# Output projections whose second accumulator runs a channel step behind the first, with no turn of the recurrence streams in the last steps of the column ahead

## The chip, the cores and the metric

The kernel runs on one core of one Trainium2 chip. A core has TensorE (PE, matrix products into the PSUM banks), VectorE (DVE), ScalarE (ACT), GpSimd (POOL, here only a queue that issues DMAs and a few memsets) and SyncE (SP, which issues the other DMAs). The engines work side by side, each through its own queue of instructions in order, and wait for one another through semaphores. The metric is the device time of one execution in microseconds (us); of several runs the median is given.

## What is computed

A decoder layer on an input of 2048 tokens by 1024 channels, in float32. What matters here is the mixer and its output projection:

```python
h = _rmsnorm(x, norm1_w[l])
proj = h @ w_in[l]                                   # 1024 -> 3840 columns
...
o_hg = _hgrn2_mixer(q_raw, f_raw, i_raw, g_raw, ...) # 4 heads of 128: gated linear recurrence
o_rw = _rwkv7_mixer(r, k, v, wd, ad, gd, ...)        # 8 heads of 64: RWKV-7 time mixing
x = x + jnp.concatenate([o_hg, o_rw], axis=-1) @ w_out[l]   # the output projection
x = x + _conv_ffn(_rmsnorm(x, norm2_w[l]), ...)
...
return _rmsnorm(x, final_norm_w)
```

## The kernel before

The tokens are cut into four blocks of 512. The first phase (`phase1`, L274) makes the input projection, both recurrences and the output projections of blocks 0, 1 and 2; the output projection of block 3 and the feed-forward part follow in the second phase. Every large product is made of three matmuls (`mm3`, L268): both operands are split into a high and a low half of a faster 32-bit format (`wh`, `wl` for weights, `hh`, `hl` for the other operand), and high by high (L270), high by low (L271) and low by high (L272) are added up in one PSUM bank. A split (`split`, L250, `split_to`, L246) is a copy on ScalarE (L254, L247) and a subtraction on VectorE (L255, L248).

Three Python generators write the instructions of phase 1. `rw_stream` (L1143) writes RWKV-7, two supersteps (`rw_super`, L700) for each block, of 42 steps each (41 in the last). `hg_stream` (L1149) writes HGRN2, four units (`hg_unit`, L999) for each block, of 16 steps each. `dense` (L555) writes the dense work: for each block 30 columns of the input projection (eight channel steps of one `mm3` each, into one bank of the tag `pj`, L663 to L679), the transposes for the next block, and the output projections. Projection 0 comes behind the columns of block 1, projection 1 behind those of block 2, and projection 2 at the end of the phase.

The order in which they write is a matter of credit. In each turn of the loop at L1173 both streams write one step. Then `fill` (L1159) gives the dense generator a credit of 2000 ns (`TICK`; times 1.5 or 0.9 in some stretches), and this writes on, paying at each `yield` the number that it yields, until the credit is used up. A column step costs 648 (436 more with a transpose), a step of an output projection 680. The order on each engine's queue is then drawn up when the program is built, from the written order and the dependences; the trace shows that it follows the written order in the main, but not everywhere.

An output projection (`out_block`, L379) has four groups: token half `i2` by column half `dh`. A group has two accumulators, each in a `pj` bank (there are two of that tag in all): `q` = 0 and 1, 128 tokens each, 512 columns. For each of eight channel steps `k` (128 channels) the weights are loaded (by POOL's queue, L393 or L399), split into `wh` and `wl` (four buffers of each, L400), and used by both accumulators, `q` = 0 first (L406 to L415). At the end of a group VectorE adds each bank to the rows of `x` (`xh`, L417), which are stored (L419). In the last group `next_block` (L474) overwrites `hh` and `hl` channel by channel with the next block's input (`split_h`, L463), and at `k` = 3 the weights of the next column are loaded ahead.

The column right ahead of projections 0 and 1 is the gate `g` of the block's last HGRN2 head. Its eviction (`ev_g`, L365) is a sigmoid on ScalarE (`sgm`) and a product on VectorE (`hgg`, L370); these free its `pj` bank. While that column runs, `next_out` (L500) splits the projection's own input, the mixer's output `oT` of two blocks earlier, into `hh` and `hl`, two channels behind the column's matmuls (L677 and L678).

The names of the streams that the text uses: `Af` and `A` are HGRN2's masked score tiles (L1059, L1085 to L1089), made from small matmuls on `hX` (L1045, L1052); `Ti` and `etmp` are RWKV-7's triangular inverse, a long chain of short VectorE operations (L850 to L856).

Of the kernel before, what the change touches and what calls it, by code (L numbers as in the profile page):

```python
# [18 lines left out]
P = 128  # L19
T = 2048  # L20
D = 1024
KD = D // P
# [45 lines left out]
def tile_layer(ctx, tc, consts, x, norm1_w, w_in, hg_lb_logits, hg_norm_w, rw_shift_mu, rw_w0, rw_w2,  # L68
# [177 lines left out]
    def split_to(hi, lo, src):  # L246
        c_ = S.copy(hi, src)  # L247
        return c_, V.tensor_sub(lo, src, hi.bitcast(F32))  # L248

    def split(pool, src, shape, name, bufs):  # L250

        hi = pool.tile(shape, F32R, tag=name + "h", name=name + "h", bufs=bufs)
        lo = pool.tile(shape, F32R, tag=name + "l", name=name + "l", bufs=bufs)
        S.copy(hi, src)  # L254
        V.tensor_sub(lo, src, hi.bitcast(F32))  # L255
        return hi, lo
# [11 lines left out]
    def mm3(acc, lhs, rhs, first, last, skip=False):  # L268
        (lh, ll), (rh, rl) = lhs, rhs
        TE.matmul(acc, lh, rh, start=first, stop=False, skip_group_check=skip)  # L270
        TE.matmul(acc, lh, rl, start=False, stop=False, skip_group_check=skip)  # L271
        TE.matmul(acc, ll, rh, start=False, stop=last, skip_group_check=skip)  # L272

    def phase1(c1):  # L274
        hp = c1.enter_context(tc.tile_pool(name="hp", bufs=1, reuse_waits="tile"))
        wp = c1.enter_context(tc.tile_pool(name="wp", bufs=2, reuse_waits="tile"))
# [17 lines left out]
        hh = hp.tile([P, KD, BLK], F32R, name="hh")  # L294
        hl = hp.tile([P, KD, BLK], F32R, name="hl")

        def bank(kind):
            return ps.tile([P, 512], F32, tag=kind, name=kind, bufs=2)
# [7 lines left out]
        def stg(tag, name, bufs):  # L306
            return sp.tile([P, BLK], F32, tag=tag, name=name, bufs=bufs)
# [71 lines left out]
        def out_block(nb, oh=None, ol=None, then=None, ahead=None):  # L379


            for i2 in range(2):
                for dh in range(2):
                    accs = [bank("pj") for _ in range(2)]
                    for k in range(KD):
                        if i2 == 0 and dh == 1 and oh is not None:
                            split_to(hh[:, k, 256:512], hl[:, k, 256:512], rows["O2"][k // 4][:, k % 4, :])
                        if k % 2 == 0:
                            part_ = 2 * i2 + dh
                            in_s = k < 6 and part_ > (0 if oh is None else 1) or k == 4 and part_ == 0 and oh is None  # L390
                            pair = (sp.tile([P, 2, 512], F32, tag=f"s{k // 2}", name="wpair") if in_s else None)
                            if in_s:
                                wload(pair, w_out[0, k * P:(k + 2) * P, dh * 512:dh * 512 + 512]  # L393
                                      .rearrange("(k p) c -> p k c", p=P))
                        if pair is not None:
                            raw = pair[:, k % 2]
                        else:
                            raw = wp.tile([P, 512], F32, tag="wraw", name="woraw", bufs=4)
                            wload(raw, w_out[0, k * P:(k + 1) * P, dh * 512:dh * 512 + 512])  # L399
                        wh, wl = split(wp, raw, [P, 512], "w", 4)  # L400
                        if k == KD - 2:
                            xh = [stg("sg", "xh", 2) for _ in range(2)]
                            for q in range(2):
                                t0 = nb * BLK + (i2 * 2 + q) * P
                                dma(xh[q], x[0, t0:t0 + P, dh * 512:dh * 512 + 512])
                        for q in range(2):  # L406
                            is_ = slice((i2 * 2 + q) * P, (i2 * 2 + q + 1) * P)
                            lhs = ((hh[:, k, is_], hl[:, k, is_]) if oh is None or i2 == 1 else
                                   (oh[k // 4][:, k % 4, is_], ol[k // 4][:, k % 4, is_]))
                            mm3(accs[q], lhs, (wh, wl), k == 0, k == KD - 1)  # L410
                            if i2 == 1 and dh == 1 and q == 1:
                                next_block(then, k)
                                if k == 3 and ahead is not None:
                                    ahead()
                            yield 680  # L415
                    for q in range(2):
                        V.tensor_add(xh[q], accs[q], xh[q])  # L417
                        r0 = (i2 * 2 + q) * P
                        (nc.gpsimd.dma_start if nb == NBLK - 2 and i2 and dh else dma)(  # L419
                            x1d[nb][r0:r0 + P, dh * 512:dh * 512 + 512], xh[q])  # L420
# [42 lines left out]
        def split_h(nb, k):  # L463

            src, w = rows[nb][:, :, k * P:(k + 1) * P], vec("n1", k)
            h4, l4 = (t_[:, k, :].rearrange("p (i t) -> p i t", i=4) for t_ in (hh, hl))
            act(h4, src, AF.Copy, scale=w)
            V.scalar_tensor_tensor(l4, src, w, h4.bitcast(F32), ALU.mult, ALU.subtract)

        def behind(k):  # L470

            return [k - 2] if 2 <= k < KD - 1 else [k - 2, k - 1, k] if k == KD - 1 else []

        def next_block(nb, k):  # L474

            if nb is not None and nb < NBLK:
                for k_ in behind(k):
                    split_h(nb, k_)
# [76 lines left out]
        def dense():  # L555
# [67 lines left out]
            ahead = iter(())  # L623
            turns = []
            for n, jb in enumerate(jobs):
                if jb[0] == "E":
                    jb[1]()
                    continue
                if jb[0] == "A":
                    if jb[1] == 0:  # L630
                        banks = spread()
                        ahead = transposed(four_tiles(rows[0]), "n1", lambda: next(banks), to_h)
                    continue
                if jb[0] == "T":
                    turns.append(jb[1])
                    continue
                if jb[0] in "OW":
                    while done["rw2"] < 2 * jb[1] + 2 or done["hg"] < 4 * jb[1] + 4:
                        yield None
                    if jb[0] == "W":  # L640
                        jb[2]()
                    else:
                        yield from (out_block(2, *rows["O"]) if jb[1] == 2 else out_block(jb[1], then=jb[1] + 2, ahead=lambda i=i: load(i)))
                    continue
                if jb[0] == "L":
                    while done["rw1"] < 2 * jb[1] + 4 or done["rw2"] < 2 * jb[1] + 2 or done["hg"] < 4 * jb[1] + 4:
                        yield None
                    (o_half if jb[1] == 2 else o_load)(jb[1])
                    continue
                _, col, ev, cond, fin = jb  # L650
                after = jobs[n + 1][1] if jobs[n + 1][0] == "O" and jobs[n + 1][1] < 2 else None
                while not cond():
                    yield None
                load(i)
                ws = loaded.pop(i)
                if i == 0:
                    next(ahead)
                    next(ahead)
                    constants()
                if jobs[n + 1][0] != "O":  # L660
                    load(i + 1)
                i += 1
                acc = bank("pj")  # L663
                then = jobs[n + 1][1] if jobs[n + 1][0] == "A" else None
                for k in range(KD):
                    wh, wl = ws[k // 4]
                    next(ahead, None)
                    mm3(acc, (wh[:, k % 4, :], wl[:, k % 4, :]), (hh[:, k, :], hl[:, k, :]), k == 0, k == KD - 1)
                    aside = k in (1, 5) and len(turns) > 0
                    if aside:  # L670
                        turns.pop(0)()
                    if k == KD - 1:
                        ev(acc)
                        if fin is not None:
                            fin()
                    next_block(then, k)
                    if after is not None:  # L677
                        next_out(after, k)  # L678
                    yield 648 + 436 * aside  # L679

        def last_dma(nb):

# [518 lines left out]
    with ExitStack() as c2:  # L1201
# [36 lines left out]
        with tc.tile_pool(name="op", bufs=1, reuse_waits="tile") as op_:  # L1238
# [61 lines left out]
            for dh in range(2):  # L1300
                accs = [pst("wacc") for _ in range(4)]
                for n, k in enumerate((0, 1, 4, 5, 2, 3, 6, 7)):
                    w = weights(k, dh)
# [15 lines left out]
                    if dh == 1 and 2 <= n:  # L1319
                        for j in range(2):  # L1320
                            q = 2 * (n - 2) + j
# [236 lines left out]
    with tc.tile_pool(name="dn", bufs=1, reuse_waits="tile") as dn:  # L1558
# [53 lines left out]
        accs = {"a": dstate["accs"]}  # L1612
# [7 lines left out]
        for s_ in range(DS, N):  # L1620
# [6 lines left out]
            if s_ < N - 3:  # L1627
                lhs, rhs = ops.pop(s_)
# [53 lines left out]
```

## Time and profile before

| | |
|---|---|
| time, median of 3 runs | 2597.45 us (2592.02, 2597.45, 2602.02) |
| the profiled execution | 2593.87 us, of which 2592.1 us from first to last instruction (the span) |
| mean granted TensorE clock | 0.997 of full speed |
| first matmul of projection 0, 1, 2 | 534.9, 856.7, 1180.0 us after the span's start |
| last matmul of projection 2 | 1258.3 us |
| matmuls of the three projections | 576 (three of 192) |

The profile's page gives busy time by engine, the costliest groups of instructions and the chain of work that ended last. The other views are answers of the trace: the waits of an engine (who waited for whom: sum in us, number, longest), the instructions of an engine in order of time (start, length in us, engine, line, operation, output `<-` inputs, shapes; in brackets the engine's idle time before it and what ended it), and the busy time of every engine in a stretch with the granted clock. A matmul's length in these rows is modelled and overlaps its neighbours'; the distance between starts tells its pace.

### The profile page before, as it was taken

The numbers are of one execution on the slowest core, as the hardware profiler recorded it, in microseconds if no ns is written. First come the engines' busy times: TensorE is split into PE (matmuls) and PEld (weight loads), VectorE is DVE, ScalarE is ACT, GpSimd is POOL, SyncE is SP. The second block draws the span as 40 slices with busy tenths as digits, with TensorE's granted clock in tenths as the row PEclk, the third lists the DMA queues.
The fourth block names the chain that finished last, engine by engine and source line by source line (L and its number), as shares of the span: only waits on it lengthen the run. The fifth ranks groups of instructions, "written<-read, shape, count | busy, mean of one in ns | idle before, by whom it ended". The sixth has DMA issues, their size and how long they took to land.

```text
span 2592.1 us, 50957 instructions
## 1 busy us (share of the span) xinstructions
PE 2526.2 (97%) x19467; PEld 2034.7 (78%) x19467; DVE 1961.6 (76%) x3744; ACT 1381.2 (53%) x2266; POOL 371.4 (14%) x660
## 2 busy tenths in 40 slices
PE   7999999999999999999999999999999999999998
PEld 6777778777777777777788888877888878888887
DVE  4878777685666866788687799988988887666555
ACT  5556554564445644355567644565555454455444
POOL 6433222222222122231000000000000000000000
PEclk9999999999999999999999999999999999999999
DMA  8846455575745657676663477757653564988655
GB/s 310 240 156 192 154 161 146 156 207 176 210 156 159 196 176 196 237 222 171 234 206 126 141 258 252 231 178 232 215 196 101 180 200 134 330 313 289 195 187 191
DMA packets 379722, 518.98 MB, mean 200 GB/s; under 512 B 113887, under 2 KB 210517, under 8 KB 379477
## 3 DMA queue, kind: packets, MB, share of 16 engines
q1 hardware_dynamic: 325361, 337.38, 41.0%
q0 software_dynamic: 54048, 178.32, 21.5%
q8 instruction: 153, 2.51, 0.4%
q14 instruction: 92, 0.75, 0.1%
q10 hardware_dynamic: 68, 0.02, 0.0%
HBM read 372.99 MB, written 134.22 MB: 196 GB/s over the span
## 4 chain that ended last, share of the span: by engine, by line
PE 58%; issue 14%; DVE 12%; DMA 6%; ACT 5%; POOL 4%; SPq 0%; POOLq 0%; DVEq 0%; ACTq 0%
PE pj L270 6%; PE pj L271 5%; PE pj L272 5%; PE ua L270 4%; PE ua L272 4%; PE ua L271 4%; PE da L270 3%; PE da L271 3%; PE da L272 3%; PE db L271 2%; PE db L272 2%; PE db L270 2%; PE ud L272 2%; PE ud L270 2%; PE ud L271 2%
## 5 line engine op out<-in xcount | busy, mean ns | idle before, releaser
L270 PE MATMUL pj<-hh,wh 128*128 128x512 f32 x960 | 394.6, 411 | 1.3 <-ACT xt L122 0.9
L271 PE MATMUL pj<-hl,wh 128*128 128x512 f32 x960 | 378.3, 394 | 0.0
L272 PE MATMUL pj<-hh,wl 128*128 128x512 f32 x960 | 378.0, 394 | 0.0
L270 PE MATMUL ua<-Bh,uwh 128*128 128x512 f32 x704 | 277.0, 393 | 4.0 <-ACT m L122 3.7
L272 PE MATMUL ua<-Bh,uwl 128*128 128x512 f32 x704 | 274.5, 390 | 1.9 <-DVE uwl L255 1.9
L271 PE MATMUL ua<-Bl,uwh 128*128 128x512 f32 x704 | 274.2, 389 | 0.0
L270 PEld LDWEIGHTS pj<-hh,wh 128*128 128x128 f32 x960 | 180.9, 189 | 47.0 <-issue 4.9
L272 PEld LDWEIGHTS pj<-hh,wl 128*128 128x128 f32 x960 | 180.9, 188 | 40.4 <-issue 1.2
L271 PEld LDWEIGHTS pj<-hl,wh 128*128 128x128 f32 x960 | 181.2, 189 | 36.2 <-issue 3.2
L254 ACT CAST uwh<-uraw 128x512 fp32r<-128x512 f32 x220 | 134.5, 617 | 132.6 <-PE ua L271 53.5
L255 DVE TENSOR_TENSOR dal<-draw,dah 128x512 fp32r<-128x512 f32 x138 | 95.2, 690 | 110.9 <-ACT dah L254 110.5
L254 ACT CAST dah<-draw 128x512 fp32r<-128x512 f32 x138 | 85.8, 622 | 164.2 <-PE da L271 77.3
L255 DVE TENSOR_TENSOR uwl<-uraw,uwh 128x512 fp32r<-128x512 f32 x220 | 147.0, 684 | 34.6 <-ACT uwh L254 34.4
L270 PEld LDWEIGHTS ua<-Bh,uwh 128*128 128x128 f32 x704 | 132.1, 188 | 35.9 <-ACT m L122 8.9
L272 PEld LDWEIGHTS ua<-Bh,uwl 128*128 128x128 f32 x704 | 132.2, 188 | 30.5 <-DVE uwl L255 2.8
L271 PEld LDWEIGHTS ua<-Bl,uwh 128*128 128x128 f32 x704 | 132.2, 188 | 26.7
L270 PE MATMUL ud<-Bh,uwh 128*128 128x512 f32 x352 | 138.0, 392 | 0.0
L272 PE MATMUL ud<-Bh,uwl 128*128 128x512 f32 x352 | 137.1, 390 | 0.0
L271 PE MATMUL ud<-Bl,uwh 128*128 128x512 f32 x352 | 137.0, 389 | 0.0
L1552 POOL DMA_DIRECT2D gd<-y x2 | 1.1, 541 | 945.9 <-DVE y L1550 945.9
L271 PE MATMUL da<-dbl,dah 128*128 128x512 f32 x332 | 129.5, 390 | 0.2 <-DVE dbl L255 0.2
L272 PE MATMUL da<-dbh,dal 128*128 128x512 f32 x332 | 129.2, 389 | 0.0
(589 smaller groups left out, 6181.1 us busy)
## 6 DMA issues: line engine op xcount, KB each, us to landing
uraw<-in_w_up_dram SPq DMA_DIRECT2D x176, 256.0 KB, 3.2
br<-gd SPq DMA_DIRECT2D x88, 256.0 KB, 4.2
draw<-Sg SPq DMA_DIRECT2D x88, 256.0 KB, 2.8
draw<-Tw SPq DMA_DIRECT2D x88, 256.0 KB, 3.8
gd<-y SPq DMA_DIRECT2D x86, 256.0 KB, 2.8
Sg<-br SPq DMA_DIRECT2D x72, 256.0 KB, 2.2
xt<-x1d SPq DMA_DIRECT2D x32, 512.0 KB, 6.6
wraw<-in_w_in_dram POOLq DMA_DIRECT2D x60, 256.0 KB, 4.8
```

The costliest lines, as they stand in the source:

```text
L254: S.copy(hi, src)
L255: V.tensor_sub(lo, src, hi.bitcast(F32))
L270: TE.matmul(acc, lh, rh, start=first, stop=False, skip_group_check=skip)
L271: TE.matmul(acc, lh, rl, start=False, stop=False, skip_group_check=skip)
L272: TE.matmul(acc, ll, rh, start=False, stop=last, skip_group_check=skip)
L1552: (dma if end is None else nc.gpsimd.dma_start)(gd_[2 * h + b][fb * P:(fb + 1) * P, :], ys[0][:, b * BLK:(b + 1) * BLK])
```

## The change

In `out_block` the second accumulator's matmuls of channel step `k` are written one step later: the order within a group was (`q` = 0, step 0), (1, 0), (0, 1), (1, 1), and so on; it becomes (0, 0), (0, 1), (1, 0), (0, 2), (1, 1), ..., (0, 7), (1, 6), (1, 7). The weights of a step are therefore kept in a dictionary until the second accumulator has used them. `next_block` and the early weight load go with the second accumulator's steps. The number of steps and what each yields stay as they were. In `dense`, the column ahead of projections 0 and 1 (`after` is set there alone) yields 0 in its steps 4 to 7, so that they cost no credit.

```diff
                     accs = [bank("pj") for _ in range(2)]
+                    ws = {}
+
+                    def step(q, k):
+                        is_ = slice((i2 * 2 + q) * P, (i2 * 2 + q + 1) * P)
+                        lhs = ((hh[:, k, is_], hl[:, k, is_]) if oh is None or i2 == 1 else
+                               (oh[k // 4][:, k % 4, is_], ol[k // 4][:, k % 4, is_]))
+                        mm3(accs[q], lhs, ws[k], k == 0, k == KD - 1)
+                        if i2 == 1 and dh == 1 and q == 1:
+                            next_block(then, k)
+                            if k == 3 and ahead is not None:
+                                ahead()
+
                     for k in range(KD):
...
-                        wh, wl = split(wp, raw, [P, 512], "w", 4)
+                        ws[k] = split(wp, raw, [P, 512], "w", 4)
...
-                        for q in range(2):
-                            is_ = slice((i2 * 2 + q) * P, (i2 * 2 + q + 1) * P)
-                            lhs = ((hh[:, k, is_], hl[:, k, is_]) if oh is None or i2 == 1 else
-                                   (oh[k // 4][:, k % 4, is_], ol[k // 4][:, k % 4, is_]))
-                            mm3(accs[q], lhs, (wh, wl), k == 0, k == KD - 1)
-                            if i2 == 1 and dh == 1 and q == 1:
-                                next_block(then, k)
-                                if k == 3 and ahead is not None:
-                                    ahead()
-                            yield 680
+                        for q, k_ in ((0, k), (1, k - 1)) + (((1, k),) if k == KD - 1 else ()):
+                            if k_ >= 0:
+                                step(q, k_)
+                                yield 680
...
                     if after is not None:
                         next_out(after, k)
-                    yield 648 + 436 * aside
+                    yield 648 + 436 * aside if after is None or k < 4 else 0
```

## The prediction

> **What bounds the kernel now.** I read the page first, then TensorE's waits, then the order of time around the longest of them.
>
> ```profile
> span 2592.1 us, 50957 instructions
> ...
> PE 2526.2 (97%) x19467; PEld 2034.7 (78%) x19467; DVE 1961.6 (76%) x3744; ACT 1381.2 (53%) x2266; POOL 371.4 (14%) x660
> ```
>
> TensorE sets the time: outside its busy time the span holds 2592.1 - 2526.2 = 65.9 us. The change neither adds nor removes an instruction, so it can only move waits and the half-clock time that follows them. Its own places are the three output projections. The answer on TensorE's waits has two rows for them:
>
> ```profile
> PE pj L270 <- DVE hgg L370: 5.4, 2, 5.0
> ...
> PE pj L270 <- DVE xh L417: 1.7, 3, 0.7
> ```
>
> The columns after the colon are the sum, the number and the longest. So the whole visible price at these places is 5.4 + 1.7 = 7.1 us, and one wait of 5.0 us is most of it. TensorE's order of time around it, at the start of the second output projection:
>
> ```profile
> 855.47 0.39 PE L272 MATMUL pj<-hh,wl 128*128 128x512 f32 x1
> 855.78 0.70 PE L1045 MATMUL hg<-hX 128*32 128x16 f32 x62
> ...
> 858.88 0.40 PE L270 MATMUL pj<-wh,hh 128*128 128x512 f32 x1
> 864.29 0.79 PE L270 MATMUL pj<-wh,hh 128*128 128x512 f32 x1 [5.01 <-DVE hgg L370]
> ```
>
> The reader should see the last matmul of the column ahead (`hh,wl`), small matmuls of an HGRN2 unit, then projection matmuls (`wh,hh`) that stop after 858.88 until the column's eviction (`hgg`) has freed its `pj` bank, which the second accumulator takes. What kept the eviction is seen on ScalarE and VectorE:
>
> ```profile
> 860.56 0.55 ACT L122 ACTIVATE Af<-hg 32x128 f32<-32x128 f32 x2 [2.55 <-DVE A L1059]
> ...
> 862.85 0.60 ACT L122 ACTIVATE sgm<-pj 128x512 f32<-128x512 f32 x1
> ```
> ```profile
> 859.13 0.68 DVE L248 TENSOR_TENSOR hl<-oraw,hh 128x512 fp32r<-128x512 f32 x1
> ...
> 859.93 0.21 DVE L1059 COPY_PREDICATED A<-cst,hg 128x64 f32<-128x64 uint32 x1
> ...
> 863.48 0.75 DVE L370 SCALAR_TENSOR_TENSOR hgg<-pj,vt,sgm 128x512 f32<-128x512 f32 x1 [0.67 <-ACT sgm L122]
> ```
>
> The column was done by about 855.9, but its sigmoid (`sgm`) stands in ScalarE's queue behind the HGRN2 copies `Af`, these wait 2.55 us for `A`, and `A` waits its turn on VectorE behind the splits of the projection's input (`hl`). So 7 us pass before `sgm` runs: a queue order, not a lack of any engine.
>
> **Part 1: the turn of the streams that goes.** A turn gives each recurrence stream one step and the dense stream 2000 ns of credit. Column steps 4 to 7 ahead of projections 0 and 1 used to cost 4 x 648 = 2592 ns; now they cost nothing. Counting the turns through the code, before: the HGRN2 step that issues these small matmuls, `A` and `Af` (unit 10, step 9) is written behind column step 7 and ahead of the projection. After: the dense stream has come two turns further, so that the same step is written ahead of column step 3, and the next step of either stream behind the projection's first four steps. Column steps 3 to 7 then lie between `Af` and `sgm`. What they are worth is seen from the half clock and the pitch behind the stall:
>
> ```profile
> 864.30:868.50 4.20, 4.20 (x12) 2.93 (x13) 3.90 (x11) 4.14 (x6) 0.54 (x1) 0.50 0.26 76
> 868.50:930.00 61.50, 60.78 (x875) 48.24 (x873) 50.93 (x123) 35.00 (x62) 10.61 (x18) 1.00 0.52 168
> ...
> 888.07 0.39 PE L271 MATMUL pj<-wl,hh 128*128 128x512 f32 x1
> 888.30 0.39 PE L272 MATMUL pj<-wh,hl 128*128 128x512 f32 x1
> ```
>
> After the wait the granted clock is 0.50 for 4.2 us in which TensorE has work: 2.1 us lost. So the stall's full price is 5.0 + 2.1 = 7.1 us. Matmuls start 0.23 us apart, so a step of three takes 0.68 us, and five column steps are 3.4 us of cover, against the 859.93 - 855.78 = 4.2 us that `A` lagged behind its matmuls' start: `Af` should be nearly out of the way when `sgm` comes. What is late next is the eviction itself. The nearest row is the first projection, where it ran almost undisturbed:
>
> ```profile
> 533.54 0.39 PE L272 MATMUL pj<-hh,wl 128*128 128x512 f32 x1
> ...
> 536.91 0.49 PE L270 MATMUL pj<-wh,hh 128*128 128x512 f32 x1 [0.34 <-DVE hgg L370]
> ```
>
> There the bank was free 536.9 - 533.8 = 3.1 us after the column's last matmul. Two steps of the first accumulator, which the lag puts ahead of the second's first, cover 1.4 us; small matmuls of the streams covered most of the rest. A stall of 0.3 us (as in this row) to 1.7 us (no small matmul moved in between) would stay in projection 1; I take 1.0, since the streams' next step is now written only four steps later but may still be drawn forward. That saves 7.1 - 1.0 = 6.1 us, with bounds 0 (`sgm` still behind `Af`) and 7.1. In projection 0 the same loss of a stream turn can turn 0.34 into 1.7: between -0.3 and +1.4, and I take +0.5.
>
> By the Trainium skill ("TensorE: Matmul & The Clock Gate", Part 1) the clock is halved only after an idle window of about 3.4 us and comes back after a busy one. By that page any stall that stays under about 3 us would carry no half-clock price; the trace agrees as far as it goes, with the 5.01 us wait followed by 0.50 and the 0.34 us wait by none.
>
> The streams lose nothing by it. Counted through, the dense stream ends in turn 359 instead of 361, and the last RWKV-7 step lies five turns ahead of that end in both. At the end of this phase the cover is:
>
> ```profile
> 1246.56 1.92 PE L991 MATMUL rw<-gdt,g 128*128 128x512 f32 x4
> ...
> 1258.32 0.39 PE L272 MATMUL pj<-wh,hl 128*128 128x512 f32 x1
> ```
>
> Some 10 us of projection matmuls, between the end of that RWKV-7 work (1246.56 + 1.92) and the last projection matmul, hide the store and reload of the last block's `oT`. Without the cover up to about 10 us would be open; with the same five turns I cost it at nothing.
>
> **Part 2: the second accumulator a step behind.** *Where it gains.* In a group the first accumulator's last matmul now has two steps (1.4 us) behind it instead of one (0.7 us). Its addition `xh` (L417) can run under these, and the next group opens with two steps on that bank. The three waits on `xh` (1.7 us) should go; as the order on VectorE decides whether the addition goes early, I take 1.2 of 0 to 1.7.
>
> *Where it costs.* The weight halves `wh` and `wl` have four buffers. A slot is freed by the second accumulator's step k-4 and first needed again by the first's step k. Six steps lay in between, now four: 4.1 us shrink to 2.7. Queued behind a later release are the cast on ScalarE, the subtraction on VectorE, and then TensorE itself. The rows of one group:
>
> ```profile
> 882.82 0.62 ACT L254 CAST wh<-wpair 128x512 fp32r<-128x512 f32 x1 [0.72 <-PE pj L272]
> ...
> 885.32 0.62 ACT L254 CAST wh<-woraw 128x512 fp32r<-128x512 f32 x1 [0.74 <-PE pj L272]
> ```
> ```profile
> 883.47 0.69 DVE L255 TENSOR_TENSOR wl<-wpair,wh 128x512 fp32r<-128x512 f32 x1 [0.20 <-ACT wh L254]
> ...
> 886.17 2.85 DVE L866 STREAM_TRANSPOSE TTs<-TZ 32x512 f32<-32x512 f32 x4
> 888.96 1.24 DVE L255 TENSOR_TENSOR wl<-woraw,wh 128x512 fp32r<-128x512 f32 x2
> ```
> ```profile
> 889.90 0.39 PE L271 MATMUL pj<-wl,hh 128*128 128x512 f32 x1
> ```
>
> Both casts begin when TensorE frees the slot (`<-PE pj L272`). With VectorE free, cast and subtraction take 884.16 - 882.82 = 1.3 us, well within 2.7. With VectorE held by transposes, the pair 885.32 to about 889.6 takes 4.3 us and left 0.3 us before its reader at 889.90. Lining up the 96 subtractions with their first readers in this way, nine have under 0.68 us to spare and eighteen under 1.36:
>
> ```profile
> L255 DVE TENSOR_TENSOR wl<-wpair,wh x52: 617/683/693, 539.9 to 1253.4; 128x512 fp32r<-128x512 f32 x52
> L255 DVE TENSOR_TENSOR wl<-woraw,wh x44: 637/682/693, 522.3 to 1255.7; 128x512 fp32r<-128x512 f32 x44
> ```
>
> The reader comes 0.68 us earlier in the order and the release 0.68 us later. Where VectorE's queue sets the time only the first counts: the nine sites lack 2.7 us together. Where the release sets it both count: the eighteen lack 11.0 us. A stall at one site gives slack to the next, so the floor is 0. I take 2.5 us, because at the tight sites of these rows it was VectorE that was late. The other moved instructions, `split_h` for the next block and the early weight load, are written one step (0.68 us) later at most and read by a column whose last step comes seven steps (4.8 us) in: nothing.
>
> **The sum.** -6.1 + 0.5 - 1.2 + 2.5 = -4.3 us. Against the profiled execution's 2593.87 us (1.8 us around its span of 2592.1) that makes 2589.6. That execution lies 3.6 us under the median 2597.45, inside the runs' 2592.02 to 2602.02; on the median the forecast is 2593.2 us.
>
> **Rivals.** *A: the stall stays.* The order on each engine is drawn up when the program is built and, as the rows show, not by source order alone: `sgm` stood behind an `Af` that is written later. If that happens again, the 6.1 us are not saved: -4.3 + 6.1 = +1.8, 2599 us. For it: nothing in the change pins `sgm`. Against: projection 0, whose eviction had no `Af` ahead of it, waited 0.34 us only.
>
> *B: slower, by the weight ring.* It decides wherever a `wl` comes more than 2.7 us after its slot's release. If the releases set most of the eighteen sites, the price is 11.0 us, which eats every gain: -6.1 + 0.5 - 1.2 + 11.0 = +4.2, 2602 us, and with the stall of A left 2608 us. For it: ScalarE's waits on `PE pj L272` at these casts. Against: 1.3 us suffice when VectorE is free.
>
> *C: nothing moves.* If the builder had already drawn the first accumulator's steps ahead, as the projection matmuls run before 858.88 suggest, the lag changes little and only noise is seen: 2597 us.
>
> **Chances.** Forecast 0.50, A 0.22, B 0.20, C 0.08. A measurement of this kernel can tell about 0.5% (13 us) from no change; none of the cases reaches that. Below 2584.5 us all gains (5.0 + 2.1 + 0.3 + 1.7 = 9.1 us) and a low draw among the runs must meet: 0.06. Above 2610.4 us B with A's stall and a high draw: 0.05. The range runs from all gains, 2588, less 4 us of the runs' spread, to B at 2602 plus 2: 2584 to 2604.
>
> **What would show it.** Right: the row `PE pj L270 <- DVE hgg L370` falls from 5.4 to under 2 us, no 0.50 clock stands near the second projection, `sgm` starts within 2 us of the column's end, the `xh` row goes, and new waits on `wl L255` or `wh L254` sum to some 2 us. Wrong: `Af` still ahead of `sgm` (A), or waits of TensorE on `wl` above 6 us (B), or a new idle stretch elsewhere between 535 and 1260 us, or in the phase's end, that I have not priced.

## The result, and the profile after

| | before | after |
|---|---|---|
| median | 2595.99 us (4 runs, 2592.02 to 2602.02) | 2619.93 us (4 runs, 2616.53 to 2621.98) |
| the profiled execution | 2593.87 us | 2617.95 us |

The changed kernel is slower: the medians lie 23.9 us apart, and the ratio estimated over the runs is 1.0082 with a 95% interval of 1.0066 to 1.0098 (some 21 us, 17 to 25). The forecast was 2593.2 us with a range up to 2604.

The page of the changed kernel first, then TensorE's waits (sum, number, longest). Behind `out_block` the lines have moved by 6, so L947 is the former L941.

```profile
span 2616.2 us, 50958 instructions
...
PE 2536.2 (97%) x19467; PEld 2043.3 (78%) x19467; DVE 1965.6 (75%) x3744; ACT 1382.5 (53%) x2266; POOL 372.7 (14%) x660
```
```profile
PE rw L956 <- DVE AR L947: 6.6, 3, 5.8
PE rw L966 <- DVE XH L973: 4.1, 1, 4.1
...
PE pj L270 <- issue: 3.5, 1, 3.5
...
PE pj L270 <- DVE xh L423: 2.3, 4, 0.8
...
PE pj L270 <- ACT wh L254: 1.8, 2, 1.1
...
PE pj L271 <- DVE wl L255: 0.3, 1, 0.3
```

The wait of 5.0 us on `hgg` is gone. In its place stand three waits that the kernel before did not have, 5.8, 4.1 and 3.5 us, none of them at a projection's accumulators. Each is followed by half clock (length, TensorE's busy time, then clock as the third number from the end):

```profile
617.40:624.20 6.80, 3.75 (x66) 3.66 (x68) 4.88 (x9) 4.03 (x14) 0.00 (x0) 0.50 0.06 24
951.90:958.70 6.80, 4.82 (x33) 3.87 (x34) 3.59 (x9) 4.93 (x15) 0.38 (x1) 0.50 0.00 0
1221.60:1231.80 10.20, 9.64 (x127) 6.60 (x131) 6.62 (x20) 2.73 (x6) 2.35 (x4) 0.50 0.35 110
```

Counting half of TensorE's busy time in these as lost gives 1.9, 2.4 and 4.8 us. So the three places cost 5.8 + 1.9, 4.1 + 2.4 and 3.5 + 4.8: 7.7, 6.5 and 8.3 us, 22.5 us together.

**The first place**, 15 us behind projection 0. VectorE's order of time, after and then before:

```profile
614.23 0.75 DVE L313 SCALAR_TENSOR_TENSOR tl<-pj,vt,tl 128x511 f32<-128x511 f32 x1 [10.62 <-ACT tl L122]
...
618.36 0.75 DVE L441 TENSOR_SCALAR xt<-xt,nst 128x1024 f32<-128x1024 f32 x1 [3.06 <-ACT nst L122]
619.02 0.68 DVE L944 TENSOR_TENSOR M<-rw,cst 128x512 f32<-128x512 f32 x1
619.62 0.68 DVE L947 TENSOR_TENSOR AR<-rw,AR 128x512 f32<-128x512 f32 x1
```
```profile
606.48 0.68 DVE L941 TENSOR_TENSOR AR<-rw,AR 128x512 f32<-128x512 f32 x1
610.93 0.75 DVE L313 SCALAR_TENSOR_TENSOR tl<-pj,vt,tl 128x511 f32<-128x511 f32 x1 [3.77 <-ACT tl L122]
...
615.51 0.75 DVE L435 TENSOR_SCALAR xt<-xt,nst 128x1024 f32<-128x1024 f32 x1 [2.67 <-ACT nst L122]
```

`tl` is the eviction of the lora column, the first column behind the projection. `xt<-xt,nst` is the row scaling of a norm: the rows of `x` that the projection has just stored are read back and normalised for the feed-forward phase, by four squares on ScalarE (`nsq`) and this scaling. `M` and `AR` are RWKV-7's. Before, the second `M` and `AR` stood ahead of `tl` and of the scaling. After, they stand behind both, and TensorE waits for them. What held `tl` is seen on ScalarE (after):

```profile
607.45 1.06 ACT L122 ACTIVATE nsq<-xt 128x1024 bf16<-128x1024 f32 x1 [7.89 <-DMA xt<-x1d]
...
612.33 1.06 ACT L122 ACTIVATE nsq<-xt 128x1024 bf16<-128x1024 f32 x1 [1.88 <-DMA xt<-x1d]
...
613.51 0.69 ACT L122 ACTIVATE tl<-pj,omu 128x512 f32<-128x512 f32 x1
614.78 1.06 ACT L122 ACTIVATE nsq<-xt 128x1024 bf16<-128x1024 f32 x1 [0.59 <-DMA xt<-x1d]
```

The squares wait for the rows to come back from memory, and `tl` stands behind two of them. Before, it stood behind two as well, but the second had its row 4 us earlier (ScalarE, before):

```profile
608.30 1.06 ACT L122 ACTIVATE nsq<-xt 128x1024 bf16<-128x1024 f32 x1 [0.81 <-DMA xt<-x1d]
...
610.23 0.67 ACT L122 ACTIVATE tl<-pj,omu 128x512 f32<-128x512 f32 x1
```

So two things differ here: the rows come later, and `M` and `AR` stand behind the scaling. `tl`'s work on VectorE ends at 615.3; had `M` followed there, it would have started 3.7 us earlier. By this estimate the place of the scaling makes the larger part of the 5.8 us. The form is that of the stall that was to be removed 250 us later: an eviction queued behind something that is waiting.

**The second place** is the same point behind projection 1. Here all four squares stand ahead of `tl` on ScalarE, and `XH`, for which TensorE waits, stands behind `tl` on VectorE, as it did before. After (two views), then before (ScalarE):

```profile
942.86 1.06 ACT L122 ACTIVATE nsq<-xt 128x1024 bf16<-128x1024 f32 x1 [8.19 <-DMA xt<-x1d]
...
949.01 1.06 ACT L122 ACTIVATE nsq<-xt 128x1024 bf16<-128x1024 f32 x1
...
952.03 0.69 ACT L122 ACTIVATE tl<-pj,omu 128x512 f32<-128x512 f32 x1
```
```profile
952.75 0.75 DVE L313 SCALAR_TENSOR_TENSOR tl<-pj,vt,tl 128x511 f32<-128x511 f32 x1 [7.59 <-ACT tl L122]
...
953.54 0.28 DVE L973 TENSOR_TENSOR XH<-rw,WC 128x128 f32<-128x128 f32 x1
```
```profile
939.69 1.06 ACT L122 ACTIVATE nsq<-xt 128x1024 bf16<-128x1024 f32 x1 [0.79 <-DMA xt<-x1d]
...
940.86 0.69 ACT L122 ACTIVATE tl<-pj,omu 128x512 f32<-128x512 f32 x1
```

**The third place** is inside projection 2, TensorE's order of time (after):

```profile
1216.63 0.40 PE L272 MATMUL pj<-wh,ohl 128*128 128x512 f32 x1
1216.96 0.78 PE L1051 MATMUL hg<-hX 128*32 128x16 f32 x66
1217.73 0.75 PE L879 MATMUL rw<-TZ,M 32*32 32x32 f32 x64
1218.41 0.24 PE L1051 MATMUL hg<-hX 128*32 128x16 f32 x4
1222.16 0.79 PE L270 MATMUL pj<-wh,ohl 128*128 128x512 f32 x1 [3.50 <-issue]
```

No semaphore is waited for. In front of the pause 134 matmuls of 16 or 32 columns stand in a row with no large one among them. (The trace has two records for each small matmul that the program writes; the 67 of an expectation below are these 134.)

### The profile page after: what moved, and what is told of

It is laid out like the page before. It is cut to its first block, busy times and chain, and to the rows that moved or that the text cites. A ratio compares the mean times of both kernels' runs of the same rounds, so it can differ in the third digit from the quotient of the medians.

```text
span 2616.2 us, 50958 instructions
## 1 busy us (share of the span) xinstructions
PE 2536.2 (97%) x19467; PEld 2043.3 (78%) x19467; DVE 1965.6 (75%) x3744; ACT 1382.5 (53%) x2266; POOL 372.7 (14%) x660
## 4 chain that ended last, share of the span: by engine, by line
PE 49%; DVE 15%; issue 14%; DMA 11%; ACT 6%; POOL 3%; SPq 1%; DVEq 0%; POOLq 0%; ACTq 0%
PE pj L270 4%; PE pj L271 4%; PE pj L272 4%; PE ua L270 4%; PE ua L272 4%; PE ua L271 4%; PE da L270 2%; PE da L271 2%; PE da L272 2%; PE ud L272 2%; PE ud L271 2%; PE ud L270 2%; PE db L271 2%; PE db L272 2%; PE db L270 2%
```

## The experiments

All of them are counted against runs of the kernel before on the same chip; the text shortens their names to e1, e2 and so on. Beside the medians the table places the difference: the same seven matmuls of the dense stream are taken in the profiled executions of a kernel and of the kernel before, and each column is what one lost against the other between two of them (us). In before's trace they stand at 497.9 us (four columns ahead of projection 0), 599.8 (the lora column behind it), 632.8 (four columns on), 856.7 (projection 1 begins), 944.1 (third column behind it), 1180.0 (projection 2 begins) and 1258.5 (the phase ends). The control, `e9_pin`, has no column over 0.6. But each column compares one execution with one. At 497.9 us, ahead of every edit, the other traces already stand 0.8 to 5.2 us behind before's, and the profiled execution lies up to 8.6 us above (`e5_third`) or 4.9 us below (`e4_pin`) its kernel's median. So a column counts where a wait in the rows explains it, and on the whole the medians decide; the intervals of the ratios, 2 to 4 us to either side, say how far they can be trusted.

| kernel | median, us | ratio, 95% | to 600 | to 633 | to 857 | to 944 | to 1180 | to 1258 |
|---|---|---|---|---|---|---|---|---|
| changed | +23.9 | 1.0066 to 1.0098 | -2.0 | +8.7 | -0.5 | +6.6 | +0.7 | +8.9 |
| e1_lag | +9.3 | 1.0025 to 1.0050 | 0.0 | +5.7 | +0.3 | +1.8 | -0.1 | +4.1 |
| e2_turn | +19.3 | 1.0064 to 1.0091 | +1.0 | +3.2 | +0.7 | +5.3 | +0.1 | +7.8 |
| e3_back | +10.9 | 1.0030 to 1.0056 | +0.2 | +5.6 | -0.5 | +1.3 | -0.1 | +4.2 |
| e4_pin | +9.4 | 1.0032 to 1.0059 | -1.7 | +1.2 | +1.7 | +1.4 | +3.6 | +3.6 |
| e5_third | +15.7 | 1.0044 to 1.0074 | -1.3 | +8.8 | -0.9 | +9.7 | +1.8 | +4.2 |
| e6_stores | +16.0 | 1.0048 to 1.0080 | -1.9 | +1.5 | +0.2 | +10.7 | +0.9 | +9.7 |
| e7_lagpin | +5.0 | 1.0013 to 1.0031 | -0.8 | 0.0 | +2.6 | +2.6 | +0.2 | +2.9 |
| e8_both | +8.3 | 1.0019 to 1.0043 | -1.5 | +1.2 | +4.6 | +2.6 | +5.2 | +1.1 |
| e9_pin | -0.5 | 0.9986 to 1.0006 | -0.1 | 0.0 | +0.6 | -0.4 | +0.5 | -0.4 |
| e10_backpin | -0.2 | 0.9990 to 1.0010 | -0.7 | +0.1 | +1.8 | +0.3 | +3.7 | +2.7 |
| e11_turnpin | +2.5 | 1.0004 to 1.0026 | +2.8 | +0.1 | -0.2 | +2.0 | +0.6 | -0.1 |
| e12_storesthird | +9.8 | 1.0024 to 1.0050 | -1.2 | +1.2 | +1.2 | +5.3 | +2.0 | +0.6 |

The first theory: the turn that the streams lose shifts them against the dense stream, and so changes the order of queues that nobody meant to touch. The rival: the lag does it, since the second addition and store come later and so the rows come back later.

**One half of the change at a time.** The lag alone is the changed kernel with the column's old price; the free steps alone are the kernel before with

```diff
-                    yield 648 + 436 * aside
+                    yield 648 + 436 * aside if after is None or k < 4 else 0
```

> The lag alone; column steps 4 to 7 ahead of the projections keep their 648 ns, so every recurrence step is written where it was before. Turn theory (the lost stream turn puts the column's norm squares and additions into other places of the queues): no stall at 607-625 us and none near 950 us, the hgg wait of 5 us may be back: -1 to +5 us against the kernel before (0.9996 to 1.002). Lag theory (the second addition and store come later, so the stored rows are loaded later, and the norm's squares stand ahead of the lora column's eviction): the two stalls of the changed kernel stay, +15 to +24 us (1.006 to 1.009). In ScalarE's program order the squares stand as before at the first place, but two of them stand ahead of Af and tl at the second, so a stall there alone would be +5 to +10 us.

> The free column steps alone, with the accumulators in step as before. ScalarE's and VectorE's program order around the two stalls is that of the changed kernel: squares ahead of Af and tl, the row scaling ahead of M and AR. Turn theory: order alone makes the stalls, +15 to +24 us against the kernel before (1.006 to 1.009). Lag theory: the rows of the last groups are stored together and land about 4 us earlier, so the squares wait 4 us less and both stalls shrink under 2 us: -4 to +5 us.

Measured: +9.3 and +19.3 us. The larger part comes with the turn, as the first theory has it, but the lag is not free, and e1 missed its +5. TensorE's waits between 535 and 1290 us, the lag and then the turn:

```profile
PE pj L270 <- DVE hgg L370: 4.9, 2, 4.5
PE hg L1126 <- DVE SH L1118: 2.1, 1, 2.1
```
```profile
PE hg L1099 <- DVE hk L1092: 4.8, 1, 4.8
PE hg L1045 <- issue: 3.8, 1, 3.8
...
PE rw L950 <- DVE AR L941: 2.6, 2, 2.2
```

The lag alone leaves the old `hgg` stall at 4.5 us. Its own loss behind projection 0 goes through `SH`, which stands behind the row scaling on VectorE. It stood so before, too. What has changed is the time, as the rival has it: the projection's last store is issued 4.1 us behind the one ahead of it instead of 0.7, and the scaling runs at 623.2 us instead of 615.5, of which 3.5 us is the distance that this trace already had. The turn alone shows the first and the third place in these rows and the second in the table (+5.3), and at projection 1 a wait for `hk` of 4.8 us in the place of the one for `hgg`. The two prices add up to more (28.6) than the change as a whole (23.9).

**The turn paid back.** With the lag and the free steps, behind the last group's stores:

```diff
+            if then is not None:
+                yield 4 * 648
```

> The changed kernel, with 4 x 648 ns of credit paid back at the end of projections 0 and 1: the column's last steps are free, but the streams get the turn before the next lora column. Turn theory: M and AR stand ahead of tl and of the row scaling on VectorE again, so the first stall falls from 5.8 to under 2 us; -4 to +8 us against the kernel before. Lag theory: the squares still wait for rows that land at 616 us, ScalarE's tl still comes behind them: the two stalls stay, +12 to +24 us.

Measured: +10.9 us, between the two. The stall behind projection 1 is nearly gone (+1.3), and projection 2 loses half of what it lost (+4.2). The first place still costs 5.6 us, now as a wait of 2.2 us for `KT`, a copy on ScalarE that stands behind three of the squares. So the turn decides about the second place and about half of the third; the other half is there with the lag alone, too. At the first, giving the turn back only changes who stands behind the squares.

**The squares held back.** The changed kernel, with the squares of this norm ordered on ScalarE behind the column that was evicted last when they are written:

```diff
-        act(sq, xt, AF.Square, accum_out=st[:, 0:1])
+        i_ = act(sq, xt, AF.Square, accum_out=st[:, 0:1])
+        if behind is not None:
+            tc.add_manual_dep(i_.ins, behind.ins.name, NOSYNC, reason="norm behind column")
```

> The changed kernel with one order written down: the norm squares of the stored rows may not stand ahead of the last evicted column on ScalarE, so all of them come behind the columns up to rkv2. No work is left out and no load is moved. If the squares that wait for the rows are what holds tl, Af, M, AR and XH, whichever edit put them there, both stalls (9.9 and 10.3 us with their half clock) go, and what is left against the kernel before is the third stall of 8.5 us less the gains inside the projections (2 + 3.6 + 0.8): 0 to +6 us. If the stalls come from M, AR and XH themselves being late by the streams' turn, they stay: +15 to +24 us.

Measured: +9.4 us. Both stalls are gone; the stretches behind projections 0 and 1 have no idle time left:

```profile
597.00:633.00 36.00, 36.00 (x436) 28.92 (x433) 14.51 (x35) 9.68 (x18) 9.58 (x18) 1.00 0.58 199
930.00:958.00 28.00, 28.00 (x372) 22.38 (x371) 12.31 (x34) 7.90 (x15) 8.51 (x16) 1.00 0.66 232
```

The squares that wait for the rows, with the scaling that needs them, are the cause at both places, whichever edit put them there. The +9.4 is more than the expected 0 to +6. One reason is a copy on ScalarE, `part`, for which TensorE now waits twice (1.2 us each at 682 and 1006 us, each with half clock behind it). The first of the two runs at 680.6 us, against 674.8 in the control; that the squares, now some 30 us ahead of it in a full queue, are what delays it is likely but was not tried. The same order on the kernel before is the control:

> The kernel before, with the norm squares of the stored rows held behind the last evicted column on ScalarE and nothing else. It is the control for the versions with that order. If holding the squares costs by itself (they come later and may hold up other evictions), it is +3 to +6 us, and then the lag with the same order (+5.0 us) costs nothing by itself. If it costs nothing (-3 to +2 us), the lag costs some 5 us by itself, and the changed kernel with both remedies (+8.3 us) carries a price of the lag and of the turn that none of the three stalls explains.

Measured: -0.5 us (0.9986 to 1.0006). Held squares cost nothing there and bring nothing.

**Late rows, or order?** The four row loads are held behind both stores in SP's queue (before, they stood so; after, the first load is between the stores of the last group behind projection 0):

```diff
-                    dma(rows[key][:, i, :], src[r0 + i * P:r0 + (i + 1) * P, :])
+                    i_ = dma(rows[key][:, i, :], src[r0 + i * P:r0 + (i + 1) * P, :])
+                    if isinstance(key, tuple):
+                        tc.add_manual_dep(i_.ins, stage["store"].ins.name, NOSYNC, reason="rows behind stores")
```

> The changed kernel, with the row loads of the stored rows held behind both stores of the projection's last group in SP's queue, as they stood before; the order on ScalarE and VectorE is left as it came. If late rows are what makes the two stalls (the second store queued behind a 512 KB load, last row 4 us later), the last row lands near 612 instead of 616 us and the stalls shrink from 5.8 and 4.1 to about 2 and 1 us, partly with their half clock: -6 to -14 us against the changed kernel (+10 to +18 us against before). If the queue order alone makes them, -4 to +1 us (+20 to +25).

Measured: +16.0 us, inside the range of the rival, but not for its reason. The first stall went entirely (+1.5), the second stayed (+10.7). VectorE's order behind projection 0 in this kernel:

```profile
612.63 0.68 DVE L946 TENSOR_TENSOR M<-rw,cst 128x512 f32<-128x512 f32 x1
613.23 0.68 DVE L949 TENSOR_TENSOR AR<-rw,AR 128x512 f32<-128x512 f32 x1
616.00 0.75 DVE L443 TENSOR_SCALAR xt<-xt,nst 128x1024 f32<-128x1024 f32 x1 [2.10 <-ACT nst L122]
```

`M` and `AR` stand ahead of the row scaling again: the pinned loads changed the order that the builder drew up on another engine. So this run is no clean test of the rows' lateness. With `tl` on ScalarE at 610.9 instead of 613.5 us, the rows' time has changed in it as well. That later rows can make a stall with the order unchanged is seen in `e1_lag`; how the 5.8 us at the first place divide between the two stays open.

**The third place.** The streams get 2 x 648 ns of credit before projection 2, in the changed kernel:

```diff
+            if oh is not None:
+                yield 2 * 648
```

> The changed kernel with one more credit step of 2 x 648 ns at the start of projection 2 alone, which moves the streams' steps there against the dense ones. In the changed kernel 67 small matmul instructions of two stream steps (hX and TZ) stand in a row without a projection matmul in TensorE's written order and 3.5 us of idle time with no wait follow; here the longest such row is 35 (before it was 40). Theory of the third stall (a dense row of small matmuls runs TensorE's instruction supply dry): the issue wait of 3.5 us and the 10 us of half clock go, -6 to -9 us against the changed kernel, so +15 to +18 us against the kernel before, with the stalls near 620 and 954 us unchanged. Rival (the third stall has another cause, such as the split of the projection's input, that the same steps carry along): +21 to +25 us.

Measured: +15.7 us, 8 less than the changed kernel, and the stretch to 1258 falls from +8.9 to +4.2. TensorE's order of time there:

```profile
1222.81 0.60 PE L1053 MATMUL hg<-hX 128*32 128x16 f32 x48
1223.34 0.50 PE L270 MATMUL pj<-wh,ohl 128*128 128x512 f32 x1
...
1224.70 0.75 PE L881 MATMUL rw<-TZ,M 32*32 32x32 f32 x64
1225.42 0.46 PE L272 MATMUL pj<-wh,ohl 128*128 128x512 f32 x1
```

The same small matmuls, now with large ones between them (rows of 48 and 64 in these lines, 70 at most there), and no pause. What is left goes with a wait of 1.2 us for `ZT` and 6.8 us of half clock from 1228.5 us. With the long row the pause went; in `e4_pin` and `e6_stores`, which keep the row of 134, it is there with 1.7 and 4.4 us. That its instructions come in too slowly fits a pause that waits for no semaphore, but was not tried, and length alone does not do it: in the changed kernel a row of 192 at 577 us has no such pause behind it, and in projection 2 of the kernel before a row of 148 at 1219 us has none.

**Two remedies together.** The squares held back and the extra credit; the stores' order and the extra credit:

> The changed kernel with both remedies: the squares held behind the last evicted column, and the credit of 2 x 648 ns at projection 2's start. With the squares alone held it was +9.4 us against the kernel before. If the third stall is independent of the first two, 3 to 6 us more go (its idle time there was 1.7 us with 3.4 us of half clock): +3 to +7 us. A version that beats the kernel before by over 0.5% is not expected of it.

> The changed kernel with the row loads held behind both stores and the 2 x 648 ns at projection 2's start. Each alone took some 7 to 9 us off the changed kernel's +24 us. If the first and the third stall are independent, both go and the second (5.3 us at 951 us with its half clock) stays: +6 to +11 us against the kernel before. If one stall's removal shifts the streams into another, +14 us or more.

Measured: +8.3 and +9.8 us. Each takes out the places that it is aimed at (e8: +1.2, +2.6, +1.1; e12: +1.2, the second place left at +5.3, +0.6), but the three are not independent. In e12 the two remedies nearly add up: 14.1 us off the changed kernel's median, against 8.2 and 7.9 singly. In e8 they do not: the squares alone had already brought projection 2 from +8.9 to +3.6, and on top of them the credit took off 1.1 us instead of 8.2. e8 came out above its range: it loses 4.6 and 5.2 us in the columns between, where `part` waits as in e4.

**What is left of lag and turn.** The lag alone with held squares; then both edits with the turn paid back and held squares, and the same without the lag:

> The lag alone, with the norm squares of the stored rows held behind the last evicted column on ScalarE. If the lag alone costs 9 us only through the squares that wait for the later rows (its stall of 2.1 us near 625 us with 6.8 us of half clock, worth 5.7 us), 3 to 7 us of them go: +2 to +6 us against the kernel before. If the lag costs by itself (weight ring, xh), it stays at +8 to +11 us.

> The changed kernel with the turn paid back at the end of projections 0 and 1 (4 x 648 ns each) and the norm squares held behind the last evicted column. Longest row of small matmul instructions in projection 2: 40, as before. If the three stalls are the whole price of the change, none is left and the gains inside projections 0 and 1 remain: -4 to +2 us against the kernel before. If lag or turn cost by themselves, +4 to +9 us.

> As the run with lag, turn paid back and held squares, but without the lag: free column steps, paid back at the end of projections 0 and 1, held squares, and the two accumulators in step. The difference to that run is the lag alone, with no stall of the rows beside it. If the lag costs nothing by itself, the two agree within 3 us; if the lag costs by itself, this one is 4 to 6 us faster than it and within 3 us of the kernel before.

Measured: +5.0, -0.2 (0.9990 to 1.0010) and +2.5 us. The second is the important one: with both edits in it, the squares out of the way and the turn given back, the kernel is as fast as before. So the price of the change lies in where the streams and the squares stand behind the projections, and no gain is left over that these medians could show (2.6 us to either side). Without the lag it is 2.7 us slower, so the lag costs nothing here; that it costs 5 us in e7 is no property of the lag alone. In the profiled executions the four kernels that have the lag and the streams' old turns (e1, e3, e7, e10) lose 2.7 to 4.2 us in projection 2, where each has a pause of 1.6 to 1.9 us, again without a semaphore, in a row of small matmuls; the control and e11 lose none there. Against that stands what the lag gains elsewhere. No version beat the kernel before.

## Why the prediction was wrong

**The stall at projection 1** (forecast -6.1 us): the row went, but not in the way forecast. `sgm` was to start within 2 us of the column's end. TensorE's order of time and ScalarE's, after:

```profile
864.09 0.39 PE L272 MATMUL pj<-hh,wl 128*128 128x512 f32 x1
...
867.65 0.50 PE L270 MATMUL pj<-wh,hh 128*128 128x512 f32 x1 [1.14 <-ACT wh L254]
869.85 1.01 PE L1105 MATMUL hg<-ident,hk 128*128 128x128 f32 x4 [1.70 <-DVE hk L1098]
```
```profile
870.95 0.60 ACT L122 ACTIVATE KT<-hg 128x512 f32<-128x512 f32 x1 [3.00 <-PE hg L1105]
871.95 0.38 ACT L122 ACTIVATE Af<-hg 64x256 f32<-64x256 f32 x1 [0.40 <-PE hg L1107]
872.23 0.58 ACT L122 ACTIVATE sgm<-pj 128x512 f32<-128x512 f32 x1
```

The column ends at 864.5 and `sgm` starts 7.8 us later, against 7.0 before: it is still held up in ScalarE's queue, now behind `KT` and a later `Af` of the same HGRN2 unit, and `KT` itself waits 3.0 us. So rival A's queue came true, one step further on, while its row did not appear: TensorE found the first accumulator's steps (the lag) and the unit's own matmuls to do, and waited for `wh` (1.1 us) and `hk` (1.7 us) in between, close enough to bring 3.4 us of half clock again:

```profile
869.98:873.38 3.40, 3.40 (x18) 2.86 (x19) 2.74 (x9) 2.01 (x4) 0.54 (x1) 0.50 0.36 131
```

That is 1.1 + 1.7 + 1.7 = 4.5 us in the place of 7.1, a gain of 2.6 and not 6.1, and the stretch to 944 us does not show even that: it lost 6.6 us, as much as the second place costs by itself. The halves agree: the lag alone left a wait of 4.5 us on `hgg`, the turn alone one of 4.8 on `hk`.

**Projection 0** (+0.5): the wait of 0.34 us for `hgg` went and one of 0.68 us for `wh` came. Over the whole stretch to 600 the profiled execution gained 2.0 us; where is not shown.

**The `xh` waits** (-1.2): wrong. They rose from 1.7 to 2.3 us. The additions were split up on VectorE, but the banks' next readers did not gain by it.

**The weight ring** (+2.5 of 0 to 11): the size, 1.8 us on `wh` and 0.3 on `wl`, is right by luck. Neither wait for `wh` comes of a slot released too late: they stand in the first steps of projections 0 and 1 (0.68 us at 538.1, 1.14 at 867.65), and at both ScalarE runs the cast of `wh` right behind the casts of the input, `hh`, without idle time between. The wait for `wl`, at 1277.6 us, lies behind all three projections. So rival B did not come true, and in the changed kernel the ring cost nothing that the rows show. With the lag alone (`e1_lag`) five such waits inside projections 0 and 1 sum to 2.5 us.

**The half clock** (no price for a wait under about 3 us, with which the trace was said to agree): the two waits that were named do agree, but the same trace has a wait of 1.28 us at 733.9 with half clock from 735.4 to 738.8. The last section has more of this.

**The step that failed** is "The streams lose nothing by it." The shift was costed at nothing, and the three places behind and in the projections cost 22.5 us by the estimate above, nearly the whole of the 23.9. The turns were counted to the end of the phase, and no loss stands there: behind 1258.5 us the changed kernel's profiled execution lost 0.3 us. What was not followed is what the shift does on the way: with the streams a step behind, three pieces of work that no edit touches (the norm squares, `M` and `AR`, and a row of small matmuls) change places in the queues behind each projection. The working did this for one place, the start of projection 1, and there too it stopped one step short of `KT`; it did not ask the same question of the next column, where a queue with a DMA wait in it was standing. Part 2 has a gap of the same kind: it costed the lag by the weight ring alone and left out that the last store of a projection comes later, and with it the rows that are read back. The prediction named "a new idle stretch elsewhere between 535 and 1260 us" as what would make it wrong: there were three. The rivals priced the wrong things, as all of them were mechanisms inside the projections.

## What to carry to other kernels

When a change shifts two instruction streams against each other, follow the shift past the place it is meant for, to the next waiting instruction in each queue: above all to one that waits for a DMA, since everything behind it waits too. A change that moves nothing but order can cost over three times the stall it removes, and the control (the same order with the shift undone) shows whether the edit or its side effect was paid for. Where a remedy is a pinned order on one engine, look at the others again: the builder can redraw them, as it did in `e6_stores`.

## What the runs showed of the hardware

The price of the half clock was taken too narrowly. The prediction had it follow only a long wait. In `e4_pin` a wait of 1.2 us is followed by it, like the one of 1.28 us in the kernel before:

```profile
681.66 0.50 PE L1149 MATMUL rw<-part,group 128*128 128x512 f32 x1 [1.22 <-ACT part L249]
```
```profile
682.20:685.60 3.40, 3.35 (x8) 2.70 (x9) 3.33 (x3) 2.54 (x4) 0.00 (x0) 0.50 0.44 165
```

So a stall of 1.2 us cost 1.2 + 1.7 us. The Trainium skill ("TensorE: Matmul & The Clock Gate", Part 1) has the clock halved after an idle window of about 3.4 us; here the wait is a third of that, and the trace decides. Not every wait of this size does it. What tells them apart in the main is how busy TensorE was over one piece of a grid. In each of the fourteen traces the stretches of half clock begin, and up to the last one end, at whole multiples of 3.41 us from each other. (In the changed kernel they begin at 617.4, 870.0, 951.9 and 1221.6 us, 74, 24 and 79 pieces of 3.41 us apart, and last 3.4, 6.8 or 10.2 us.) From 100 us on, half clock set in 64 times, and each time TensorE had been busy for less than 0.67 of the piece just before, by the lengths in the rows; ahead of the stretch in `e4_pin` it was 0.57. Of the 43 pieces at full clock with TensorE busy for less than half, 39 were followed by half clock; of the 9958 with 0.7 or more, none. In between both occur. So in these traces a wait's price depends on what other idle time falls into the same piece, and on where the grid happens to lie.

Long rows of small matmuls (under 128 columns) can end in a pause with no semaphore behind it: 134 of them and 3.5 us in the changed kernel, 156 and 3.8 in `e2_turn`, 208 and 1.5 at 757 us in the kernel before. Between 100 and 1300 us of the fourteen traces, 30 of the 35 such pauses over 0.5 us stand in or behind a row of 134 or more; most rows of 128 to 192 have none. What else it takes stays open.
